# Stick-breaking prompt attention: where a unit's sigmoids stand against the copies of an older unit, and which unit carries the output projection

## The chip, the cores and the metric

The kernel runs on one core of one Trainium2 chip. The metric is device microseconds (us) of one execution. The engines named below are PE (TensorE, matrix products and transposes), DVE (VectorE), ACT (ScalarE), POOL (GpSimd) and SP (the queue that issues most DMAs). Each engine works through its own instructions in the order in which they were written for it; between engines there are only semaphores.

## The reference, cut to what matters

One step of a hybrid decoder layer: a prompt of 4096 tokens and eight short samples pass a common input projection, four branches (state space, short convolution, stick-breaking attention, attention to a memory), gates and an output projection. The change lies in the stick-breaking attention of the prompt (4 heads of 64, strictly causal):

```python
z = einsum("nqhd,nkhd->nhqk", q, k) * HEAD_DIM ** -0.5 + bias
log_beta = log_sigmoid(z)
log_1m = where(mask, log_sigmoid(-z), 0.0)
rev = cumsum(log_1m, axis=3, reverse=True)
excl = concatenate([rev[..., 1:], 0])
wts = where(mask, exp(log_beta + excl), 0.0)
out = einsum("nhqk,nkhd->nqhd", wts, v)
```

The kernel works without logarithms: a weight is sigmoid(z) times the product of sigmoid(-z) over all later keys, and that product is a scan from the last key to the first.

## The kernel before, in words

Up to about 1950 us the kernel projects the prompt and decodes the samples; that part is not touched. Then comes the attention loop. Its blocks are (query chunk of 512, head pair, key chunk of 512), from the diagonal key chunk backwards; each block has four *units* of 128 queries, in all 288 units. Of the 72 blocks 16 are diagonal, and their units have 128, 256, 384 and 512 keys; all others have 512. For unit `i` the loop body (lines 1882 to 1910) does, with `j = i - 3`:

- `scores(i)` (L1451, L1455): PE makes the scores z of both heads, six matmuls. The tag `z` has 4 buffers in PSUM, so two units' worth.
- background pieces (`run_bg`) and `out_step`: `run_bg` advances generators, of which `sample_gen` (the rest of the sample decoding, with its own transposes in the tag `wt`) is the largest; `out_step` advances the output projection `out_unit` (L1561 to L1563, tile `wo`). One step is six matmuls; after four steps half a tile of 128 tokens is done and DVE adds the residual (`yb`). Some 27 of the 32 tiles of 128 tokens are projected inside the loop, on average 1.5 steps for every two units. In `before` both run in odd units.
- `stage_b(j)` (L1489): PE transposes the weights of the older unit `j` (tag `wt`, 2 buffers in PSUM, one per head); the copy into `wT` is made by DVE for head 0 (L1492) and by ACT for head 1; every fourth unit ACT makes both. For those units `j` is even.
- `weights(i)`: for each head ACT makes `om` = sigmoid(-z) and `bt` = sigmoid(z), DVE scans `om` into `T` (L1472), POOL multiplies `bt` by `T` and, except in the last key chunk, copies the carry (`cy`, L1477). `om` has one buffer per head, `T` 4, `bt` 7.
- `run_norms`: the final norm of a projected tile, in pieces.
- `stage_c` (L1505): if `j` is even, so if `i` is odd, PE multiplies the values with the weights of the two units before `j` (tile `ya`).

So every odd unit of `before` holds scores, projection, transposes and values on PE, every even unit only scores and transposes. The order of the Python calls is the order of the instructions on each engine; a buffer is handed on when the instructions that used it are done.

Of the kernel before, what the change touches and what calls it, by code (L numbers as in the profile page):

```python
# [29 lines left out]
def hymba_kernel(ctx: ExitStack, tc: tile.TileContext, x_p, x_s, cache_k, cache_v, s_re, s_im, s_conv,  # L30
# [10 lines left out]
    def act(out, in_, f=AF.Copy, **kw):  # L41
        return S.activation(out, in_, f, **kw)  # L42

    def tt(eng, out, a, b, op):
        return eng.tensor_tensor(out=out, in0=a, in1=b, op=op)  # L45
# [58 lines left out]
    def run_bg(skip=None):  # L104
        for g in list(bg):
            if g is not skip and next(g, "end") == "end":
                bg.remove(g)
# [1011 lines left out]
    def load_q(qc, hp):  # L1119
        t = x_tile("qst", F32R).rearrange("p (l n) -> p l n", l=2)  # L1120
        SP.dma_start(t.bitcast(F32), qscr[:, hp * 128:(hp + 1) * 128, qc * 512:(qc + 1) * 512].rearrange("l p n -> p l n"))
        qst_t[qc, hp] = t
# [186 lines left out]
    i = 0  # L1309
# [96 lines left out]
    def load_kv(*b):  # L1406
        load_keys(*b, sb.tile([128, 2, 512], F32R, tag="kst", name="kst", bufs=2))
        load_v2(*b)
# [8 lines left out]
    def wout_gen():  # L1417
        for k in range(KT):
            stg = sb.tile([128, DM], F32, tag="x2", name="stg2", bufs=2)
            SP.dma_start(stg, w_out[0, k * 128:(k + 1) * 128, :])  # L1420
            act(wo[:, k, 0, :], stg)
            tt(V, wo[:, k, 1, :], stg, wo[:, k, 0, :].bitcast(F32), ALU.subtract)
            yield
# [17 lines left out]
    def scores(qc, hp, kb, qt):  # L1441
        ks = kst_t[qc, hp, kb]
        diag = kb == qc
        n = (qt + 1) * 128 if diag else 512

        qs = qst_t[qc, hp]
        zs = [ztile() for h in range(2)]
        for lq_, lk in ((0, 0), (0, 1), (1, 0)):
            for h in range(2):
                r = slice(64 * h, 64 * h + 64)  # L1450
                mm(zs[h][:, 0:n], qs[r, lq_, qt * 128:(qt + 1) * 128], ks[r, lk, 0:n],  # L1451
                   start=(lq_ + lk == 0), stop=(lq_ == 1 and not diag))
        if diag:
            for h in range(2):
                mm(zs[h][:, n - 128:n], idr, maskr, start=False, stop=True)  # L1455
        return zs, n

    def weights(zs, n, qc, hp, kb, qt):
        diag = kb == qc
        ws = []  # L1460
        for h in range(2):
            z, hd = zs[h], 2 * hp + h
            om = om2[h]
            T = sb.tile([128, 513], F32, tag="T2", name="T2", bufs=4)
            c = cy[:, 2 * qt + h:2 * qt + h + 1]
            bt = sb.tile([128, 512], F32, tag="bt2", name="bt2", bufs=7)
            act(om[:, 0:n], z[:, 0:n], AF.Sigmoid, scale=-0.125, bias=nb4[:, hd:hd + 1])
            act(bt[:, 0:n], z[:, 0:n], AF.Sigmoid, scale=0.125, bias=b4[:, hd:hd + 1])
            if n < 512:
                V.memset(om[:, n:n + 1], 1.0)  # L1470

            V.tensor_tensor_scan(T[:, 0:n + 1][:, ::-1], om[:, 0:n + 1][:, ::-1],  # L1472
                                 z[:, 0:1].to_broadcast([128, n + 1]), 1.0 if diag else c,
                                 op0=ALU.mult, op1=ALU.bypass)
            tt(P, bt[:, 0:n], bt[:, 0:n], T[:, 1:n + 1], ALU.mult)
            if kb:
                P.tensor_copy(c, T[:, 0:1])  # L1477
            ws.append(bt)
        return ws, n
# [3 lines left out]
    def stage_b(qt, ws, n):  # L1483

        for h in range(2):
            t = wtp()
            cnt[0] += 1
            for k in range(n // 128):
                tr(t[:, k, :], ws[h][:, k * 128:(k + 1) * 128], ident)  # L1489
            if qt % 2 == 0:  # L1490
                wts[h] = sb.tile([128, 4, 2, 128], F32, tag="wT2", name="wT2", bufs=4)
            (act if h or cnt[0] % 8 == 1 else V.tensor_copy)(wts[h][:, 0:n // 128, qt % 2, :], t[:, 0:n // 128, :])  # L1492
        return dict(wts)

    def stage_c(qc, hp, kb, qt, wTs):

        if kb == qc and qt == 1:
            ya[0] = ps.tile([128, 512], F32, tag="ya", name="ya", bufs=1)
        v = vt_t[qc, hp, kb]
        nk = qt + 1 if kb == qc else 4  # L1500
        for k in range(nk):

            q0 = qt if kb == qc and k == nk - 1 else qt - 1
            for h in range(2):
                mm(ya[0][h * 64:h * 64 + 64, q0 * 128:(qt + 1) * 128], v[:, k, h * 64:h * 64 + 64],  # L1505
                   wTs[h][:, k, q0 - qt + 1:2, :].rearrange("p a b -> p (a b)"),
                   start=(kb == qc and qt == 1 and k == 0), stop=(kb == 0 and k == nk - 1),
                   skip_group_check=True)
        if kb == 0 and qt == 3:
            y = Yc.setdefault(qc, sb.tile([128, 2, 512], F32, tag="Yc", name="Yc", bufs=1) if hp == 0 else None)  # L1510
            act(y[:, hp, :], ya[0])
            sq = sb.tile([128, 512], F32, tag="sq2", name="sq2", bufs=2)
            act(sq, ya[0], AF.Square)
            sqs2.append(sq)
            if hp == 1:
                bg.append(merge_c(qc, y, list(sqs2)))
                sqs2.clear()
# [78 lines left out]
    def run_norms():  # L1596
        for g in list(nrm):
            if next(g, "end") == "end":
                nrm.remove(g)
# [12 lines left out]
    def out_step(n):  # L1612

        ost["acc"] += n
        while ost["acc"] >= 1.0:
            if ost["gen"] is None:
                if ost["nxt"] is None:
                    out_ready()
                    ost["acc"] = min(ost["acc"], 1.0)
                    return ost["nxt"] is not None  # L1620
                ost["gen"], ost["nxt"] = ost["nxt"], None
                if not ost["split"]:
                    next(ost["gen"])
                ost["split"] = False
                out_ready()
            ost["acc"] -= 1.0
            ost["done"] += 1
            if ost["done"] % 8 == 6 and ost["nxt"] is not None and not ost["split"]:
                next(ost["nxt"])
                ost["split"] = True  # L1630
            if next(ost["gen"], "end") == "end":
                ost["gen"] = None
            if ost["done"] % 4 == 0 and not ost.get("tail"):
                break
        return True
# [240 lines left out]
    units = [(qc, hp, kb, qt) for (qc, hp, kb) in blocks for qt in range(4)]  # L1876
    nu = len(units)
    smp = sample_gen()
    bg.append(smp)
    sa, sbq = {}, {}  # L1880
    LAG = 3
    for i in range(nu + LAG + 1):
        j = i - LAG
        z = None
        if i < nu:
            qc, hp, kb, qt = units[i]
            if qt == 0:
                bi = i // 4
                if bi + 1 < len(blocks):
                    load_kv(*blocks[bi + 1])  # L1890
                    if blocks[bi + 1][:2] != (qc, hp):
                        load_q(*blocks[bi + 1][:2])
            z = scores(*units[i])
        if i == 5:
            bg.append(wout_gen())

        if i % 2 or i < 20:
            run_bg(smp if i < 10 or i % 2 == 0 else None)
        if i < nu:
            if i % 2:  # L1900
                out_step(max(0.0, 8.0 * (4 * NCH - 5) - ost["done"]) * 2 / (nu - i + 1))

        if 0 <= j < nu:
            ws, n = sa.pop(j)
            sbq[j] = stage_b(units[j][3], ws, n)
        if z is not None:
            sa[i] = weights(*z, *units[i])
        run_norms()
        if j >= 2 and j % 2 == 0:
            stage_c(*units[j - 1], sbq[j - 1])  # L1910
# [46 lines left out]
```

## Time and profile before

| what | value |
|---|---|
| median of three runs | 3369.91 us (3361.84 to 3379.39) |
| the profiled execution | 3368.33 us |
| its span | 3366.6 us, so 1.7 us lie around it |
| mean granted TensorE clock | 0.977 |
| PE busy over the span | 3155.7 us (94%) |
| DVE, ACT, POOL busy | 2290.5 (68%), 1783.4 (53%), 1267.8 us (38%) |

Durations below are read from the one profiled execution. In the timeline a row gives the start, the length, the engine, the line and operation, the tile written and read, how many instructions were merged, and in brackets the idle time before it with what ended it. A matmul's end is modelled; the distance between the starts of two groups tells what a group cost.

### The profile page before, as it was taken

Reading aid. Unit: us, or ns where it says so; the run is one execution under the profiler, and the core shown is the slowest. Engines: PE = TensorE matmul, PEld = TensorE weight load, DVE = VectorE, ACT = ScalarE, POOL = GpSimd, SP = SyncE. Lnnn points to the kernel's source line nnn. Section 1 sums busy time; section 2 is a strip of 40 time slices with the busy share of each in tenths; the row PEclk is TensorE's granted clock in tenths of the full one; section 3 lists DMA queues with packets and bytes.
Section 4 is the critical chain, followed back from the end, with each engine's and each line's share of the span. In section 5 each row is a group of like instructions: output and inputs, shape, how many; then the busy total and the mean of one; then the engine's idle time right before and its main releaser. Section 6 shows DMA issues by size and latency. Waiting matters only on the chain. (4 is left out here: it accounts for less than half of the span.)

```text
span 3366.6 us, 64925 instructions
## 1 busy us (share of the span) xinstructions
PE 3155.7 (94%) x23191; PEld 2260.2 (67%) x23191; DVE 2290.5 (68%) x3659; ACT 1783.4 (53%) x3324; POOL 1267.8 (38%) x1721
## 2 busy tenths in 40 slices
PE   7888999999999999999999978999999998999998
PEld 6556767677767677776677656666676665666667
DVE  5876667666676676676756567777767777677773
ACT  3435444443544444444434456667656666677771
POOL 1466422222222122222223035555545455555550
PEclk9999999999999999999999989999999999999999
DMA  6667887888887879878887443333333233322213
GB/s 212 193 209 235 276 276 227 270 280 268 277 262 244 283 250 299 266 234 271 270 276 223 147 160 122 97 97 92 98 94 96 72 106 101 96 77 85 87 60 119
DMA packets 382178, 623.55 MB, mean 185 GB/s; under 512 B 54568, under 2 KB 245488, under 8 KB 381856
## 3 DMA queue, kind: packets, MB, share of 16 engines
q1 hardware_dynamic: 344912, 484.90, 45.8%
q0 software_dynamic: 36944, 134.50, 12.1%
q8 instruction: 185, 3.03, 0.4%
q14 instruction: 137, 1.12, 0.1%
HBM read 539.33 MB, written 79.95 MB: 184 GB/s over the span
## 5 line engine op out<-in xcount | busy, mean ns | idle before, releaser
L45 POOL TENSOR_TENSOR bt<-bt,T 128x512 f32<-128x512 f32 (+3 forms) x576 | 603.3, 1047 | 605.7 <-DVE T L1472 416.5
L215 PE MATMUL pj<-xh,whl 128*128 128x512 f32 (+1 forms) x1792 | 725.0, 405 | 0.0
L1472 DVE TENSOR_TENSOR_SCAN T<-om,cy,z 128x513 f32<-128x513 f32 x448 | 549.7, 1268 | 231.5 <-ACT bt L42 100.4
L217 PE MATMUL pj<-xh,whl 128*128 128x512 f32 (+1 forms) x1792 | 659.8, 368 | 8.2 <-DVE whl L45 8.2
L216 PE MATMUL pj<-xh,whl 128*128 128x512 f32 (+1 forms) x1792 | 657.2, 367 | 0.1
L890 POOL DMA_INDIRECT kt<-in_cache_sb_k_dram,idxk x256 | 299.7, 1171 | 890.9 <-DVE kT L1058 790.5
L215 PEld LDWEIGHTS pj<-xh,whl 128*128 128x128 f32 x1792 | 344.5, 192 | 118.1 <-issue 79.8
L42 ACT ACTIVATE wT<-wt 128x512 f32<-128x512 f32 (+3 forms) x360 | 195.2, 557 | 408.1 <-PE wt L1489 407.9
L217 PEld LDWEIGHTS pj<-xh,whl 128*128 128x128 f32 x1792 | 343.9, 192 | 69.3 <-DVE whl L45 11.5
L42 ACT ACTIVATE bt<-z,b 128x512 f32<-128x512 f32 (+3 forms) x576 | 385.1, 669 | 0.0
L42 ACT ACTIVATE om<-z,nb 128x512 f32<-128x512 f32 (+3 forms) x576 | 380.4, 660 | 2.7 <-PE z L1455 2.1
L216 PEld LDWEIGHTS pj<-xh,whl 128*128 128x128 f32 x1792 | 346.2, 193 | 45.4 <-issue 8.6
L1451 PE MATMUL z<-kst,qst 64*128 64x512 f32 (+3 forms) x1704 | 325.2, 423 | 54.1 <-DVE T L1472 51.8
L1489 PE MATMUL wt<-ident,bt 128*128 128x128 f32 x2112 | 299.6, 281 | 34.9 <-ACT wT L42 8.0
L1058 DVE STREAM_TRANSPOSE kT<-kt 128x1024 f32<-128x1024 f32 x256 | 315.2, 1233 | 12.7 <-DMA kt<-in_cache_sb_k_dram,idxk 11.8
L1489 PEld LDWEIGHTS wt<-ident,bt 128*128 128x128 f32 x2112 | 241.5, 143 | 105.4 <-issue 52.2
L45 DVE TENSOR_TENSOR whl<-stg,whl 128x1024 fp32r<-128x1024 f32 x191 | 233.8, 1224 | 106.9 <-ACT whl L42 105.5
L1451 PEld LDWEIGHTS z<-kst,qst 64*128 64x128 f32 x1704 | 160.6, 187 | 176.5 <-DVE T L1472 95.0
L1505 PE MATMUL ya<-wT,vt 128*64 128x256 f32 (+1 forms) x2176 | 263.2, 383 | 0.3 <-DVE wT L1492 0.3
L42 ACT ACTIVATE whl<-stg 128x1024 fp32r<-128x1024 f32 x192 | 203.1, 1058 | 83.1 <-issue 34.9
L1561 PE MATMUL wo<-wo,mt 128*128 128x512 f32 x512 | 217.9, 426 | 2.3 <-ACT mt L42 2.3
L1563 PE MATMUL wo<-wo,mt 128*128 128x512 f32 x512 | 204.7, 400 | 1.0 <-DVE mt L45 1.0
(755 smaller groups left out, 4848.6 us busy)
## 6 DMA issues: line engine op xcount, KB each, us to landing
vt<-in_cache_sb_v_dram SPq DMA_DIRECT2D x1024, 128.0 KB
stg<-in_w_in_dram SPq DMA_DIRECT2D x192, 512.0 KB
kst<-kscr SPq DMA_DIRECT2D x71, 512.0 KB
xt<-in_x_prompt_dram SPq DMA_DIRECT2D x64, 512.0 KB
pkt<-pack_d SPq DMA_DIRECT2D x64, 449.0 KB
vt<-vscr SPq DMA_DIRECT2D x71, 256.0 KB
mr<-mscr SPq DMA_DIRECT2D x32, 512.0 KB
out_dram<-yb SPq DMA_DIRECT2D x32, 512.0 KB
```

The lines of the kernel that those rows point to most:

```text
L42: return S.activation(out, in_, f, **kw)
L45: return eng.tensor_tensor(out=out, in0=a, in1=b, op=op)
L215: mm(o[:, t0:t1], hi[:, k, :], xh[:, k, 0, t0:t1], start=(k == 0), stop=False)
L216: mm(o[:, t0:t1], hi[:, k, :], xh[:, k, 1, t0:t1], start=False, stop=False)
L217: mm(o[:, t0:t1], lo[:, k, :], xh[:, k, 0, t0:t1], start=False, stop=(k == KT - 1))
L890: P.indirect_dma_start(out=kq[j], out_offset=None, in_=ck_rows, in_offset=bass.IndirectOffsetOnAxis(ap=idxk[:, u // NU, gg:gg + 1], axis=0))
L1058: V.transpose(kts[j], kq.pop(j))
L1451: mm(zs[h][:, 0:n], qs[r, lq_, qt * 128:(qt + 1) * 128], ks[r, lk, 0:n], start=(lq_ + lk == 0), stop=(lq_ == 1 and not diag))
L1472: V.tensor_tensor_scan(T[:, 0:n + 1][:, ::-1], om[:, 0:n + 1][:, ::-1], z[:, 0:1].to_broadcast([128, n + 1]), 1.0 if diag else c, op0=ALU. ...
L1489: tr(t[:, k, :], ws[h][:, k * 128:(k + 1) * 128], ident)
L1505: mm(ya[0][h * 64:h * 64 + 64, q0 * 128:(qt + 1) * 128], v[:, k, h * 64:h * 64 + 64], wTs[h][:, k, q0 - qt + 1:2, :].rearrange("p a b -> p ...
L1561: mm(o, mt[:, k, 0, :], wo[:, k, 0, cs], start=(k == 0), stop=False)
```

## The change

In the loop body the background pieces and the output projection move from odd units to even ones; the values stay in odd units. And `weights(i)`, with its sigmoids, scans and products, is called before `stage_b(j)`, with its transposes and copies, instead of after it. Nothing is added or removed; every number of buffers stays.

```diff
-        if i % 2 or i < 20:
-            run_bg(smp if i < 10 or i % 2 == 0 else None)
+        if i % 2 == 0 or i < 20:
+            run_bg(smp if i < 10 or i % 2 else None)
         if i < nu:
-            if i % 2:
+            if i % 2 == 0:
                 out_step(max(0.0, 8.0 * (4 * NCH - 5) - ost["done"]) * 2 / (nu - i + 1))
-
+        if z is not None:
+            sa[i] = weights(*z, *units[i])
         if 0 <= j < nu:
             ws, n = sa.pop(j)
             sbq[j] = stage_b(units[j][3], ws, n)
-        if z is not None:
-            sa[i] = weights(*z, *units[i])
         run_norms()
         if j >= 2 and j % 2 == 0:
             stage_c(*units[j - 1], sbq[j - 1])
```

The places shown are in the last query chunk, in blocks off the diagonal. First ACT; the numbers behind the names tell one buffer's use from another, and a semaphore in brackets names the engine that is waited for. Before, from the copies of an odd unit on:

```order
L42 ACTIVATE wT2_35435<-wt_35430 128x4x128 [waits PE_49]
L42 ACTIVATE wT2_35442<-wt_35437 128x4x128 [waits PE_49]
L42 ACTIVATE om2_0_23883<-z_35409,nb4_87 128x512 [waits DVE_49]
L42 ACTIVATE bt2_35445<-z_35409,b4_86 128x512 [waits Pool_49]
L42 ACTIVATE om2_1_23884<-z_35410,nb4_87 128x512 [waits DVE_49]
L42 ACTIVATE bt2_35452<-z_35410,b4_86 128x512 [waits Pool_49]
```

Now, an even unit (z 35369 and 35370, with the transposes wt 35410 and 35416 of the unit three older) and the start of the odd one:

```order
L42 ACTIVATE om2_0_23883<-z_35369,nb4_87 128x512 [waits DVE_49,PE_49]
L42 ACTIVATE bt2_35397<-z_35369,b4_86 128x512 [waits Pool_49]
L42 ACTIVATE om2_1_23884<-z_35370,nb4_87 128x512 [waits DVE_49,PE_49]
L42 ACTIVATE bt2_35404<-z_35370,b4_86 128x512 [waits PE_49,Pool_49]
L42 ACTIVATE wT2_35361<-wt_35416 128x4x128 [waits PE_49]
L42 ACTIVATE om2_0_23883<-z_35422,nb4_87 128x512 [waits DVE_49,PE_49]
```

The four sigmoids stood behind the copies and stand ahead of them now; the second `bt` has a wait for PE that it did not have.

DVE at the same place, before: an even unit, then an odd one whose copies are both ACT's (the two rr rows belong to a background piece):

```order
L1492 COPY wT2_35346<-wt_35382 128x4x128 [waits PE_49]
L1472 SCALAR_TENSOR_TENSOR T2_35394<-om2_0_23883,cy_23887,z_35374 128x513 [waits DVE_49,Activation_49]
L1472 SCALAR_TENSOR_TENSOR T2_35401<-om2_1_23884,cy_23887,z_35375 128x513 [waits DVE_49,Activation_49]
L286 TENSOR_REDUCE rr2_35420<-rt_35417 128x4 [waits PE_49]
L288 TENSOR_SCALAR rr2_35420<-rr2_35420 128x4 [waits DVE_49]
L1472 SCALAR_TENSOR_TENSOR T2_35444<-om2_0_23883,cy_23887,z_35409 128x513 [waits Activation_49,Pool_49]
L1472 SCALAR_TENSOR_TENSOR T2_35451<-om2_1_23884,cy_23887,z_35410 128x513 [waits Activation_49,Pool_49]
```

and now, an even unit (T 35396, 35403), an odd one whose copies are both ACT's, and the next even one with the addition `yb` of the projection:

```order
L1472 SCALAR_TENSOR_TENSOR T2_35396<-om2_0_23883,cy_23887,z_35369 128x513 [waits Activation_49,Pool_49]
L1472 SCALAR_TENSOR_TENSOR T2_35403<-om2_1_23884,cy_23887,z_35370 128x513 [waits Activation_49,Pool_49]
L1492 COPY wT2_35355<-wt_35410 128x4x128 [waits PE_49]
L1472 SCALAR_TENSOR_TENSOR T2_35430<-om2_0_23883,cy_23887,z_35422 128x513 [waits Activation_49,Pool_49]
L1472 SCALAR_TENSOR_TENSOR T2_35437<-om2_1_23884,cy_23887,z_35423 128x513 [waits Activation_49,Pool_49]
L45 TENSOR_TENSOR yb_35298<-wo_35299,xt2_34808 128x512 [waits DMAHW7_49,PE_49]
L1472 SCALAR_TENSOR_TENSOR T2_35485<-om2_0_23883,cy_23887,z_35470 128x513 [waits DVE_49,Activation_49,Pool_49]
L1472 SCALAR_TENSOR_TENSOR T2_35492<-om2_1_23884,cy_23887,z_35471 128x513 [waits DVE_49,Activation_49,Pool_49]
L1492 COPY wT2_35449<-wt_35499 128x4x128 [waits PE_49]
```

The copy of a unit's transposes stood ahead of its two scans and stands behind them; `yb` stands ahead of an even unit's scans.

PE before, an odd unit: scores, projection, transposes (the values follow):

```order
L1451 MATMUL z<-kst,qst 128x512 [waits DVE_49] x2
L1451 MATMUL z<-kst,qst 128x512 x4
L1561 MATMUL wo<-wo,mt 128x512
L1562 MATMUL wo<-wo,mt 128x512
L1563 MATMUL wo<-wo,mt 128x512
L1561 MATMUL wo<-wo,mt 128x512
L1562 MATMUL wo<-wo,mt 128x512
L1563 MATMUL wo<-wo,mt 128x512
L1489 MATMUL wt<-ident,bt_35395 128x128 [waits DVE_49,Pool_49]
L1489 MATMUL wt<-ident,bt_35395 128x128 x3
L1489 MATMUL wt<-ident,bt_35402 128x128 [waits Activation_49,Pool_49]
L1489 MATMUL wt<-ident,bt_35402 128x128 x3
```

and now, the end of an even unit (projection, transposes) and an odd one (scores, transposes, values):

```order
L1562 MATMUL wo<-wo,mt 128x512
L1563 MATMUL wo<-wo,mt 128x512
L1489 MATMUL wt<-ident,bt_35235 128x128 [waits DVE_49,Pool_49]
L1489 MATMUL wt<-ident,bt_35235 128x128 x3
L1489 MATMUL wt<-ident,bt_35242 128x128 [waits DVE_49,Pool_49]
L1489 MATMUL wt<-ident,bt_35242 128x128 x3
L1451 MATMUL z<-kst,qst 128x512 x6
L1489 MATMUL wt<-ident,bt_35307 128x128 [waits Activation_49,Pool_49]
L1489 MATMUL wt<-ident,bt_35307 128x128 x3
L1489 MATMUL wt<-ident,bt_35314 128x128 [waits DVE_49,Pool_49]
L1489 MATMUL wt<-ident,bt_35314 128x128 x3
L1505 MATMUL ya<-wT_35355,vt_34892 64x256
```

The scores lose their own wait for DVE. Between the transposes of an even unit and those of the odd unit after it there are now only six score matmuls, and the second four transposes of the odd unit wait for DVE.

## Rows read from the trace of the kernel before

**Rows 1.** Windows: stretch, busy us of PE, PEld, DVE, ACT, POOL, clock, DMA.

```profile
1958.00:2050.00 92.00, 70.74 (x392) 45.77 (x393) 59.28 (x102) 60.10 (x126) 42.14 (x58) 0.78 0.51 168
2050.00:3290.00 1240.00, 1165.88 (x7485) 793.99 (x7484) 903.06 (x1159) 842.95 (x1532) 678.52 (x1004) 0.99 0.29 90
```

**Rows 2.** Waits, 1980 to 3290 us: total us, times, longest.

```profile
ACT wT L42 <- PE wt L1489: 404.8, 270, 9.3
DVE T L1472 <- ACT bt L42: 141.7, 107, 3.4
...
PE z L1451 <- DVE T L1472: 51.5, 143, 1.2
```

**Rows 3.** Timeline of PE, one pair of units late in the loop.

```profile
3203.65 0.97 PE L1451 MATMUL z<-kst,qst 64*128 64x512 f32 x6
...
3204.55 1.09 PE L1489 MATMUL wt<-ident,bt 128*128 128x128 f32 x8
...
3205.57 0.50 PE L1451 MATMUL z<-kst,qst 64*128 64x512 f32 x1
...
3206.23 0.96 PE L1451 MATMUL z<-kst,qst 64*128 64x512 f32 x5 [0.16 <-DVE T L1472]
...
3207.12 0.50 PE L1561 MATMUL wo<-wo,mt 128*128 128x512 f32 x1
...
3208.62 1.03 PE L1489 MATMUL wt<-ident,bt 128*128 128x128 f32 x8
...
3209.58 1.95 PE L1505 MATMUL ya<-wT,vt 128*64 128x256 f32 x16
...
3211.46 0.96 PE L1451 MATMUL z<-kst,qst 64*128 64x512 f32 x6
```

**Rows 4.** Timeline of ACT and DVE, same pair.

```profile
3202.94 0.69 ACT L42 ACTIVATE bt<-z,b 128x512 f32<-128x512 f32 x1
...
3203.72 2.46 DVE L1472 TENSOR_TENSOR_SCAN T<-om,cy,z 128x513 f32<-128x513 f32 x2 [1.59 <-ACT bt L42]
...
3209.25 1.09 ACT L42 ACTIVATE wT<-wt 128x512 f32<-128x512 f32 x2 [0.66 <-PE wt L1489]
```

**Rows 5.** Timeline of DVE and PE, an odd unit with a sample piece.

```profile
2700.02 2.44 DVE L1472 TENSOR_TENSOR_SCAN T<-om,cy,z 128x513 f32<-128x513 f32 x2
...
2701.16 0.60 PE L1489 MATMUL wt<-ident,bt 128*128 128x128 f32 x4
...
2702.39 0.66 DVE L1801 COPY g<-wt 128x512 f32<-128x512 f32 x1
...
2702.97 0.68 DVE L1492 COPY wT<-wt 128x512 f32<-128x512 f32 x1
...
2703.19 0.63 PE L1489 MATMUL wt<-ident,bt 128*128 128x128 f32 x4 [1.43 <-DVE g L1801]
...
2703.75 1.95 PE L1505 MATMUL ya<-wT,vt 128*64 128x256 f32 x16
```

**Rows 6.** Timeline: transposes and the addition of a projected half.

```profile
2121.70 1.03 PE L1489 MATMUL wt<-ident,bt 128*128 128x128 f32 x8
2121.89 0.69 DVE L45 TENSOR_TENSOR yb<-wo,xt 128x512 f32<-128x512 f32 x1 [1.04 <-PE wo L1563]
```

**Rows 7.** Timeline of PE: an odd unit's scores, after a pair with short values.

```profile
3169.64 0.49 PE L1451 MATMUL z<-kst,qst 64*128 64x512 f32 x1 [0.39 <-DVE T L1472]
...
3171.71 0.51 PE L1561 MATMUL wo<-wo,mt 128*128 128x512 f32 x1
```

**Rows 8.** Timeline of PE: late second transposes of odd units, first and last.

```profile
2113.93 0.63 PE L1489 MATMUL wt<-ident,bt 128*128 128x128 f32 x4 [0.78 <-ACT wT L42]
...
3036.16 0.63 PE L1489 MATMUL wt<-ident,bt 128*128 128x128 f32 x4 [1.11 <-POOL cy L1477]
```

**Rows 9.** Windows as in rows 1; a projection step's start and end.

```profile
2600.00:2620.00 20.00, 17.05 (x90) 11.22 (x86) 15.64 (x18) 10.89 (x20) 10.03 (x10) 0.83 0.35 118
2840.00:2860.00 20.00, 16.46 (x110) 10.72 (x110) 15.06 (x22) 14.61 (x27) 10.41 (x17) 1.00 0.49 155
...
2341.40 0.78 PE L1561 MATMUL wo<-wo,mt 128*128 128x512 f32 x1
...
2343.83 1.04 PE L1489 MATMUL wt<-ident,bt 128*128 128x128 f32 x8
```

## The prediction, made before the changed kernel ran

> **What bounds the kernel now.** I read the windows first, then the waits, then the timeline of single pairs of units. Off the attention loop the two programs are alike, so only the loop counts. Its steady stretch of 1240 us has PE busy for 1166, DVE for 903, ACT for 843 and POOL for 679 [rows 1]. PE is the engine to watch, but no engine is full, so the order decides. Of the waits, ACT's copies wait 405 us in all for PE's transposes, and what stands behind these copies on ACT, the four sigmoids, waits with them; DVE's scans wait for the last `bt` sigmoid; and at the end of this chain PE waits 143 times for a scan before it may write scores [rows 2]. The timeline tells what one such time costs: the pair of units at 3203.65 spends 0.90 us on the even unit's scores, 1.02 on its transposes, 1.55 on the odd unit's scores, 1.50 on one projection step, 0.96 on transposes and 1.88 on values, together 7.81 [rows 3]. The odd scores start, stop after one matmul for the scan that frees their buffer and go on: 0.65 us more than the even ones. Without that the pair is 7.16.
>
> **What goes.** Sigmoids no longer stand behind copies that wait for the projection, so the scans of a unit are over long before the scores two units later want its buffer. The even unit's scans now end about 3 us after its transposes start (below), the scores that want them come 6 us after. 143 x 0.65 = 93 us go [rows 2, 3]. After the 14 pairs with short values (a block behind a diagonal one) the odd scores are longer, 2.07 from start to projection instead of 1.55 [rows 7]: 14 x 0.5 = 7. Together 100.
>
> The second thing that goes is a collision with the sample pieces. Before, such a piece sits in an odd unit; PE transposes for it, but DVE comes to copy only after the even unit's two scans, and meanwhile the piece holds one of the two `wt` buffers. In the example the second transposes start at 2703.19, 2.03 us after the first, where 0.49 would do [rows 5]. There are 30 such odd units (late by 0.4 us or more), the first and the last in [rows 8]; summed over them PE loses 29 us. Now the piece sits in an even unit, at a time when DVE has done the odd unit's copy and waits for the next sigmoids (by steps like those below, some 1.7 us). I let 29 go, and also 12 for even units whose transposes came 0.4 us or more late (18 of them, the same way of counting), and 10 for projection steps that ran at the lower clock behind such gaps (2.43 instead of 1.50 in the example [rows 3, 9]). These 51 are the softest numbers here; I leave 12 of them standing, since some pieces have waits of their own. So 100 + 39 = 139 us go.
>
> **What comes.** The wait to price is the new one in the ACT rows of the change. `bt` has 7 buffers and a unit takes two. Calling `weights(i)` before the transposes of unit i-3 makes eight live, so the second `bt` of every unit waits until PE has transposed head 0 of unit i-3. Queued behind that sigmoid are ACT's copy and, through the scan of head 1, DVE's copy of head 0; and for this copy waits the second half of the next unit's transposes. In an even unit PE has only six score matmuls in between. Step by step, from the start of the even unit's transposes:
>
> - to ACT's start: 0.63 (3208.62 to 3209.25 [rows 3, 4])
> - sigmoid: 0.69, and 0.09 to the scan (3203.63 to 3203.72 [rows 4])
> - scan of head 1, to the start of what follows on DVE: 1.17 (two scans take 2.37 to the next start, 2700.02 to 2702.39 [rows 5], the first about 1.20 of it)
> - copy 0.68; 0.14 from a copy's end to PE (2703.05 to 2703.19 [rows 5])
>
> Sum 3.40. Without waiting PE would be there after 0.97 (rest of the even transposes) + 0.90 (scores) + 0.51 (first half) = 2.38 [rows 3]. The wait is 1.02, and four transposes restarted after a wait take 0.56 until the values start instead of 0.51 [rows 5]: 1.06 us per pair. In the odd unit the same chain has 1.88 us of values, 0.90 of scores and 1.50 of projection as cover, 4.3 us, and costs nothing. A longer projection step doesn't help the even unit: the chain starts at its end.
>
> 288 units in 72 blocks, 16 of them diagonal, are 112 full pairs and 32 diagonal ones. 112 x 1.06 = 119 us. The second pair of a diagonal block has 384 keys in its even unit and a short transpose in the odd one: shorter sigmoid, scan and cover, by the same chain about 0.7; 16 x 0.7 = 11. The first pair has 128 keys: nothing.
>
> `yb`, moved along with the projection, stands ahead of the even unit's scans on DVE and waits for the last projection matmul: it starts 0.19 after the transposes and takes 0.69 [rows 6]. Then 0.88 + 1.20 + 1.17 + 0.68 + 0.14 = 4.07 instead of 3.40: 0.67 more. It happens twice for each of 27 tiles, by share 42 times in full pairs: 28 us. The subtraction for `mt`, the norm pieces and most sample pieces fall into DVE's gap between its copy and the next scans; if that cover is too short, they delay the scans as `yb` does, which I hold inside the 12 us above. DMAs, SP's queue and POOL's products keep their places; POOL has half its time free.
>
> **Sum**, against the profiled execution's own 3368.3 us (1.6 below the median of the runs): 3368.3 - 139 + 119 + 11 + 28 = 3387 us. A change of 0.5% (17 us) is about what a measurement of this kernel can tell from none, and the sum stands just at that edge. Bounds of what no row shows directly: the new wait could be 0.8 (scan and copy overlapping more) or 1.4 us (a late sigmoid) per pair, so 26 us less or 38 more; the soft 51 all gone or half left, 12 less or 14 more.
>
> **Rivals.**
>
> *The waits go and little comes in their place.* If the second `bt` did not hold up the scans, in a pair with one projection step (about half) DVE's copy would still be 0.7 late, 56 x 0.7 = 39, and with two steps in time: 3368 - 139 + 39 + 13 (half of the `yb` cost) = 3281. For it: PE's waits on scans are all of one kind, and these do go. Against it: seven buffers for eight live tiles, and the scan is seen to start right behind the `bt` sigmoid and not behind `om` [rows 4]. Chance 0.15.
>
> *One wait for another, and no change.* If the soft 51 go wholly and the `yb` cost is hidden wherever two steps are taken (half): 3387 - 12 - 14 = 3361, with the upper bound of the wait up to 3380. For it: the terms are of like size, and what they count is the same DVE and ACT work pushed from one buffer to the other. Against: `yb` always ends a call of the projection, so nothing hides it. Chance 0.23.
>
> *Slower, by the clock.* The clock granted to PE fell to 0.83 in a stretch with several waits in a row and stayed at 1.00 in another with PE busy for only 16.5 of 20 us [rows 9]. Now every pair holds a gap of about 1 us, with `yb` of 1.7. If half of the 144 pairs ran one step's length at the lower of the two levels (1.2 for 2.4 GHz) and lost 0.93 as the step shown [rows 3, 9], that is 67 us: 3454. Against: that second stretch; by these two rows it takes several gaps close together. Chance 0.12.
>
> [...]
>
> **How the numbers follow.** The forecast, 3387, has 0.50, with its own range 3365 to 3410: 0.22 of it within 0.5% and 0.28 above. The first rival (0.15) is faster, and 0.03 of the second; the rest of the second (0.20) is the same; the third (0.12) slower. Faster 0.18, same 0.42, slower 0.40. The range from 3320 to 3440 leaves out most of the first rival and half of the third, about 0.2.
>
> **What would show it.** In the new profile PE's waits for scans before scores should be gone, and the odd unit's transposes, 1.0 us long before, should take about 2.1, with their second half waiting for DVE's copy; the even unit's second `bt` should start 0.63 after the transposes start. Late in the loop, where the sample is done, a pair with one step should take 8.2 us instead of 7.8; the middle, from 2100 to 3030, should gain. The forecast is wrong if odd transposes stay at 1.0 (then the first rival), if the clock of the loop falls below 0.95 (the third), or if even units' transposes begin to wait, which I took to be free.

## The result, and the profile after

The changed kernel takes 3430.8 us (median; 3419.1 to 3434.9), the kernel before 3369.0 in the same series: ratio 1.0175, 95% interval 1.0153 to 1.0196. The forecast was 3387 with an own range up to 3410, so the direction of the sum was right and its size too small by 44 us. The profiled execution took 3433.7 us, its span is 3431.9.

First the windows of the changed kernel, columns as in [rows 1]. The last two stretches are ten us around a late pair and two pairs without one.

```profile
2050.00:3290.00 1240.00, 1084.82 (x7112) 736.11 (x7112) 870.47 (x1117) 822.77 (x1466) 623.34 (x963) 0.98 0.29 88
...
3066.00:3076.00 10.00, 6.61 (x34) 3.97 (x33) 8.90 (x9) 5.16 (x11) 4.76 (x7) 0.71 0.22 84
3244.00:3262.00 18.00, 15.66 (x110) 10.18 (x108) 13.12 (x15) 13.52 (x23) 10.60 (x19) 1.00 0.25 75
```

In the same 1240 us PE is busy for 1085 us, where it was 1166 [rows 1]; DVE, ACT and POOL do less too. So nobody is busier: everybody waits. The clock explains little of it: 0.98 against 0.99, by estimate 0.01 of 1240 us or some 12 us. Who waits for whom stands in the list of waits from 1980 to 3350 us (us in total, times, longest):

```profile
ACT bt L42 <- PE wt L1489: 184.7, 125, 3.9
PE wt L1489 <- DVE wT L1492: 147.7, 129, 3.8
...
DVE T L1472 <- ACT bt L42: 109.1, 86, 3.9
...
DVE yb L45 <- PE wo L1563: 102.2, 51, 5.8
...
DVE Yc L1533 <- DMA ev<-gscr: 21.2, 9, 4.8
```

The 143 waits of PE for a scan before scores [rows 2] are gone; no such line is left. In their place PE waits 129 times before transposes for DVE's copy, 1.1 us each time, and ACT 125 times before a `bt` sigmoid for transposes. How one hangs on the other shows in the timeline of the pair at 3244.45, with one step of projection, like that of [rows 3]:

```profile
3246.83 1.03 PE L1489 MATMUL wt<-ident,bt 128*128 128x128 f32 x8
3247.53 0.69 ACT L42 ACTIVATE bt<-z,b 128x512 f32<-128x512 f32 x1 [0.23 <-PE wt L1489]
3247.80 0.97 PE L1451 MATMUL z<-kst,qst 64*128 64x512 f32 x6
...
3248.31 1.28 DVE L1472 TENSOR_TENSOR_SCAN T<-om,cy,z 128x513 f32<-128x513 f32 x1 [0.21 <-ACT bt L42]
...
3248.85 0.63 PE L1489 MATMUL wt<-ident,bt 128*128 128x128 f32 x4
...
3249.51 0.67 DVE L1492 COPY wT<-wt 128x512 f32<-128x512 f32 x1
...
3250.32 0.63 PE L1489 MATMUL wt<-ident,bt 128*128 128x128 f32 x4 [0.84 <-DVE wT L1492]
...
3250.88 1.95 PE L1505 MATMUL ya<-wT,vt 128*64 128x256 f32 x16
...
3252.76 0.96 PE L1451 MATMUL z<-kst,qst 64*128 64x512 f32 x6
...
3255.13 1.03 PE L1489 MATMUL wt<-ident,bt 128*128 128x128 f32 x8
3255.33 0.69 DVE L45 TENSOR_TENSOR yb<-wo,xt 128x512 f32<-128x512 f32 x1 [2.72 <-PE wo L1563]
...
3255.94 2.45 DVE L1472 TENSOR_TENSOR_SCAN T<-om,cy,z 128x513 f32<-128x513 f32 x2
...
3259.11 0.63 PE L1489 MATMUL wt<-ident,bt 128*128 128x128 f32 x4 [1.33 <-DVE wT L1492]
```

Read it downwards: even transposes, second `bt` 0.70 later, scan of head 1, copy of head 0, second half of the odd transposes. From 3246.83 to 3250.32 this is 3.49 us. The odd transposes take 2.03 us from their start to that of the values (3248.85 to 3250.88) instead of 1.0; the pair takes 8.31 us instead of 7.81. In the next pair `yb` stands ahead of both scans; there the wait grows from 0.84 to 1.33 and the pair to 8.79. Pairs with two steps went from 9.2 to 9.7, with three from 10.6 to 11.0 (medians). Summed over 140 pairs the loop takes 1362.6 us (1975.4 to 3338.0), before 1300.7 (1972.6 to 3273.2): 61.9 of the 65.4 us between the two profiled executions lie here.

One kind of pair the forecast had put at next to nothing. Timeline around 3062.74, where a chunk is finished and its norm (`merge_c`) begins:

```profile
3066.43 0.75 DVE L1533 SCALAR_TENSOR_TENSOR Yc<-Yc,gnc,ev 128x512 f32<-128x512 f32 x1 [4.83 <-DMA ev<-gscr]
...
3067.85 0.75 DVE L1533 SCALAR_TENSOR_TENSOR Yc<-Yc,gnc,ev 128x512 f32<-128x512 f32 x1 [0.67 <-DMA ev<-gscr]
3068.53 2.45 DVE L1472 TENSOR_TENSOR_SCAN T<-om,cy,z 128x513 f32<-128x513 f32 x2
...
3071.43 0.88 PE L1489 MATMUL wt<-ident,bt 128*128 128x128 f32 x3 [3.14 <-DVE wT L1492]
...
3072.24 1.55 PE L1505 MATMUL ya<-wT,vt 128*64 128x256 f32 x8
```

A product that waits for a tile just ordered by DMA now stands ahead of an even unit's scans. The scans start more than 2 us late, PE waits 3.14 us, and then runs at the lower of its two levels: these values take 1.48 us to the next scores (3072.24 to 3073.72) where the same number took 0.80 elsewhere, and the window above shows 0.71. The lower level also stands behind shorter waits, as here, behind one of 1.39 us:

```profile
2540.96 0.38 PE L1489 MATMUL wt<-ident,bt 128*128 128x128 f32 x1 [1.39 <-DVE wT L1492]
2541.26 3.50 PE L1505 MATMUL ya<-wT,vt 128*64 128x256 f32 x16
```

These values take 3.44 us to the next scores, elsewhere 1.88. In sixteen odd units the values ran wholly or in part at the lower level, in the kernel before in three.

### The profile page after: what moved, and what is told of

Same layout as the page of the kernel before. It is cut to its first block, busy times and chain, and to the rows that moved or that the text cites. A ratio compares the mean times of both kernels' runs of the same rounds, so it can differ in the third digit from the quotient of the medians.

```text
span 3431.9 us, 65412 instructions
## 1 busy us (share of the span) xinstructions
PE 3122.5 (91%) x23191; PEld 2236.2 (65%) x23191; DVE 2303.4 (67%) x3659; ACT 1803.9 (53%) x3324; POOL 1241.7 (36%) x1721
## 3 DMA queue, kind: packets, MB, share of 16 engines
q14 instruction: 140, 1.15, 0.1%
## 5 line engine op out<-in xcount | busy, mean ns | idle before, releaser
L45 POOL TENSOR_TENSOR bt<-bt,T 128x512 f32<-128x512 f32 (+3 forms) x576 | 585.9, 1017 | 686.1 <-DVE T L1472 552.1
L1489 PE MATMUL wt<-ident,bt 128*128 128x128 f32 x2112 | 315.9, 281 | 180.0 <-DVE wT L1492 148.6
L42 ACT ACTIVATE bt<-z,b 128x512 f32<-128x512 f32 (+3 forms) x576 | 375.1, 651 | 189.3 <-PE wt L1489 184.7
L1505 PE MATMUL ya<-wT,vt 128*64 128x256 f32 (+1 forms) x2176 | 277.3, 398 | 0.3 <-DVE wT L1492 0.3
L1451 PE MATMUL z<-kst,qst 64*128 64x512 f32 (+3 forms) x1704 | 268.3, 420 | 1.6 <-DMA qst<-qscr 1.6
L1561 PE MATMUL wo<-wo,mt 128*128 128x512 f32 x512 | 213.8, 418 | 0.6 <-ACT mt L42 0.6
L1505 PEld LDWEIGHTS ya<-wT,vt 128*64 128x64 f32 x2176 | 150.8, 143 | 90.5 <-issue 34.9
L1563 PE MATMUL wo<-wo,mt 128*128 128x512 f32 x512 | 201.2, 393 | 0.5 <-DVE om L1470 0.5
L1562 PE MATMUL wo<-wo,mt 128*128 128x512 f32 x512 | 200.9, 392 | 0.0
```

What stands on the lines that cost most here:

```text
L1561: mm(o, mt[:, k, 0, :], wo[:, k, 0, cs], start=(k == 0), stop=False)
```

## The experiments

Times are medians, ratios are to the kernel before, measured beside each, with 95% intervals. Runs of different series are compared by their ratios.

**Each half alone.** `parity` moves projection and pieces to the even units and leaves `stage_b` ahead of `weights`; `order` puts `weights` ahead and leaves projection and pieces in odd units.

> Only the projection and the pieces move to the unit without values; transposes and copies stay ahead of the sigmoids, as before. Theory (each half alone costs, and the two are joined by the order on ACT): the even unit's sigmoids now wait behind copies that come only after the projection, so the scans end about 1 us too late for the scores two units later, in every pair; 3400 to 3480 us, PE waiting for scans before scores in 250 or more places. Rival (the place of the projection matters little, all of the loss is in the new order of sigmoids and copies): 3360 to 3380 us.

> Only the sigmoids, scans and products go ahead of the transposes and copies; projection and pieces stay in the unit with values. Theory (what costs is that the second bt of the even unit waits for transposes that stand behind the projection): here these transposes follow the scores at once, the second bt hardly waits, and a pair with two steps of projection covers the chain; 3320 to 3385 us, odd transposes late by 1.1 to 1.6 us only in pairs with one step. Rival (DVE's copy behind its scans costs the same with either place of the projection): 3415 to 3445 us.

`parity`: 3361.3 us, 0.9970 (0.9954 to 0.9986). `order`: 3346.1 us, 0.9935 (0.9916 to 0.9954). So neither half costs; both gain a little, and only together they lose. For `parity` my theory was wrong: PE does wait for scans before nearly all even scores (first row below, 0.5 us each), but nearly all odd scores lost their wait, and the late transposes behind sample pieces are nearly gone. The time is the rival's, but its reason is not: the new order alone loses nothing. For `order` the theory held but for a size: the odd transposes wait in pairs with one step (the other rows, 0.63 us where 1.1 to 1.6 were expected; such pairs take 7.98) and not in pairs with two (8.51, against 9.2 before).

Waits of `parity`:

```profile
PEld z L1451 <- DVE T L1472: 77.4, 149, 1.1
```

Timeline of `order`, an odd unit's transposes, one step:

```profile
3225.69 0.60 PE L1489 MATMUL wt<-ident,bt 128*128 128x128 f32 x4
...
3226.11 0.66 DVE L1492 COPY wT<-wt 128x512 f32<-128x512 f32 x1
...
3226.91 0.63 PE L1489 MATMUL wt<-ident,bt 128*128 128x128 f32 x4 [0.63 <-DVE wT L1492]
```

**Eight buffers for `bt`.**

```diff
-        return sb.tile([128, 512], dt, tag="ev2", name=name, bufs=4)
+        return sb.tile([128, 512], dt, tag="ev2", name=name, bufs=3)
...
-            bt = sb.tile([128, 512], F32, tag="bt2", name="bt2", bufs=7)
+            bt = sb.tile([128, 512], F32, tag="bt2", name="bt2", bufs=8)
```

> The changed kernel with eight buffers for bt instead of seven (the tag ev2 gives one of its four for it). Theory (seven buffers for eight live tiles): the wait of the second bt for the transposes goes; a pair with one step gains the 0.23 us that ACT waited there, a pair with two steps, where the transposes come 1.5 us later, all of its 1.15: 3345 to 3385 us. Rival (the sigmoids, scans and copy in a row are too long by themselves, the buffer is incidental): 3405 to 3425 us, that is 112 x 0.23 = 26 us less at most.

3373.8 us, 1.0013 (1.0003 to 1.0023): 1.6% or 55 us of the loss go. The price per pair is as expected: with two steps 9.69 becomes 8.53, with three 11.05 becomes 9.89, with one 8.31 becomes 7.98 (medians); pairs with `yb` gain nothing (one step 8.80 and 8.81, two steps 10.2 and 10.4). A pair with two steps, timeline:

```profile
3188.85 2.45 DVE L1472 TENSOR_TENSOR_SCAN T<-om,cy,z 128x513 f32<-128x513 f32 x2
...
3189.22 0.70 ACT L42 ACTIVATE bt<-z,b 128x512 f32<-128x512 f32 x1
...
3190.27 1.03 PE L1489 MATMUL wt<-ident,bt 128*128 128x128 f32 x8
3191.23 0.66 DVE L1492 COPY wT<-wt 128x512 f32<-128x512 f32 x1
...
3192.13 1.09 PE L1489 MATMUL wt<-ident,bt 128*128 128x128 f32 x8
```

The second `bt` starts a microsecond before the transposes that it had to wait for, the copy follows both scans while PE makes the odd scores, and the odd transposes run in one piece. So the buffer is the whole wait with two steps, and about 0.3 of 1.15 us with one; there the two scans, one behind the other, still make the copy late. The list of waits also fits that neither half loses alone. In `order` the even transposes follow the scores at once, and no even unit's second `bt` waits for them; those of odd units do, 83 times and 140 us in all, where values and scores lie behind as cover. In `parity` the transposes of the older unit are issued ahead of the sigmoids, so eight buffers are never wanted, and no `bt` waits for transposes.

**The scan without the `bt` sigmoid.** The scan's second operand is never used (its operation is a bypass), but it is read from the scores, which the sigmoid reads too, and the scan starts only behind that sigmoid.

```diff
-                                 z[:, 0:1].to_broadcast([128, n + 1]), 1.0 if diag else c,
+                                 nb4[:, hd:hd + 1].to_broadcast([128, n + 1]), 1.0 if diag else c,
```

> The changed kernel, with the scan's unused second operand (its second operation is a bypass) taken from a column in SBUF instead of the scores in PSUM; by that the scan no longer waits for the bt sigmoid, only for om. Theory (scan 1 and DVE's copy hang on the second bt): without yb the copy comes 0.9 us sooner and the odd transposes wait 0.0 to 0.3 us instead of 0.84; where yb stands ahead of the scans nothing is gained; 70 x 1.15 + 16 us less: 3320 to 3355 us. Rival (the copy's place behind two scans is what costs, whatever they wait for): the scans start sooner but odd transposes still wait 0.7 us or more in pairs with one step, 3390 us or more. If the scan is slower with both operands in SBUF (1.28 us now), the gain shrinks by that.

3429.7 us, 1.0177 (1.0158 to 1.0196): nothing gained, the rival's number. But this tells little of the chain, since the edit brought a cost of its own. Window and timeline of this run:

```profile
2050.00:3290.00 1240.00, 1083.58 (x7107) 741.39 (x7104) 1012.48 (x1117) 825.11 (x1468) 976.82 (x960) 0.97 0.29 88
```

```profile
3238.09 2.13 POOL L45 TENSOR_TENSOR bt<-bt,T 128x512 f32<-128x512 f32 x1
...
3243.92 3.71 DVE L1472 TENSOR_TENSOR_SCAN T<-om,cy,nb 128x513 f32<-128x513 f32 x2
...
3244.38 1.12 POOL L1477 COPY cy<-T 128x1 f32<-128x1 f32 x1
...
3258.30 0.18 POOL L1477 COPY cy<-T 128x1 f32<-128x1 f32 x1
...
3258.44 2.45 DVE L1472 TENSOR_TENSOR_SCAN T<-om,cy,nb 128x513 f32<-128x513 f32 x2
...
3259.89 1.89 POOL L45 TENSOR_TENSOR bt<-bt,T 128x512 f32<-128x512 f32 x1 [1.41 <-DVE T L1472]
```

Beside a scan POOL's copy of one column takes 1.12 us instead of 0.18, and two scans take 3.71 us here and up to 4.34 elsewhere, instead of 2.45. In the last rows the scans take 2.45 as ever; there POOL's product, which begins beside them, takes 1.89 instead of 1.09. POOL's busy time rose from 623 to 977 us.

**Copy between the scans.** With seven buffers and `yb` in its place, only DVE's copy of head 0 is moved. PE's order stays.

```diff
+            if h == 0 and mid is not None:
+                mid()
...
-            sa[i] = weights(*z, *units[i])
+            sa[i] = weights(*z, *units[i], mid=copies)
```

(`copies` calls `stage_b` for the older unit; ACT's copies are issued after `weights`, as before.)

> The changed kernel, seven bt buffers, with DVE's copy of head 0 between the two scans instead of behind both; yb stays ahead. Theory (PE waits only for this copy; the second bt and the scan of head 1 may come late): the copy needs one scan and the transposes, so odd transposes are not late with one step or two, and 0.2 to 0.4 late with yb; 145 + 21 us of the odd scores and transposes go, 15 stay: 3265 to 3310 us. Rival (the scan of head 1, now behind the copy, comes late instead, and PE waits for scans before scores again): 3350 us or more.

3286.9 us, 0.9763 (0.9747 to 0.9780): 139 us below the changed kernel. This is the theory's number. Its waits:

```profile
ACT bt L42 <- PE wt L1491: 153.6, 119, 3.7
...
PE wt L1491 <- DVE wT L1499: 34.4, 61, 4.2
```

It settles the main point. The second `bt` waits nearly as often as in the changed kernel (119 times against 125), but PE's wait for the copy falls from 148 to 34 us: the second `bt` and the scan of head 1 may be late, what costs is the copy.

**`yb` behind scans and copy**: with seven buffers (`yb`), with eight (`bt8_yb`), and with the copy between the scans (`mid_yb`).

```diff
-            tt(V, yb[0:rows, cs], o[0:rows], xt[0:rows, cs], ALU.add)
+            def add(o=o, cs=cs, half=half):
+                tt(V, yb[0:rows, cs], o[0:rows], xt[0:rows, cs], ALU.add)
...
+        for f in later:
+            f()
```

> The changed kernel, seven bt buffers, copy behind both scans, and only yb moved behind scans and copy. This sizes the yb term alone, forecast as 42 x 0.67 = 28 us. Theory (with seven buffers yb falls partly together with the wait of the second bt, so it costs less here than the 55 us that it cost with eight): 20 to 35 us less than the changed kernel, 3396 to 3412 us. Rival (the terms add up, as if each stood alone): 50 us or more less, 3380 us.

> The changed kernel with eight bt buffers, and yb written on DVE behind the unit's scans and copy instead of ahead of them. In the run with eight buffers alone pairs with yb stay at 8.80 us (one step) where those without take 7.98, and 10.40 against 8.53 with two steps. Theory (yb ahead of the scans pushes DVE's copy back, and with it the odd transposes): 36 x 0.8 + 17 x 1.2 + 9 us of diagonal pairs, 58 us less than 3374: 3305 to 3330 us. Rival (yb costs its own 0.67 us, whereever it stands, because DVE's row of scans and copy is full): 3350 to 3375 us.

> As the run before (copy between the scans, seven buffers), and yb behind scans and copy. Theory: the last 0.2 to 0.4 us of the pairs with yb go, and pieces of the scan delay in the pairs after them; 10 to 20 us below the run with the copy between the scans. Rival (yb there is already hidden): the same within 5 us.

`yb`: 3394.4 us, 1.0075 (1.0058 to 1.0092), 34 us less than the changed kernel. `bt8_yb`: 3318.9 us, 0.9850 (0.9833 to 0.9867), 55 us less than with eight buffers alone, and its pairs with `yb` take 7.98 like those without. `mid_yb`: 3271.2 us, 0.9706 (0.9688 to 0.9724), 16 to 19 us less than `mid`. All three are as the theory had them (`yb` 2 us below its range): what `yb` costs depends on what else is late in that pair.

**The chunk norm's products two pieces later.**

```diff
+            sls.append(sl)
...
-            V.scalar_tensor_tensor(y[:, ft, :], y[:, ft, :], gnc[:, 4 + ft:5 + ft], sl, op0=ALU.mult, op1=ALU.mult)
         yield
+        yield
+        for ft in range(2):
+            V.scalar_tensor_tensor(y[:, ft, :], y[:, ft, :], gnc[:, 4 + ft:5 + ft], sls[ft], op0=ALU.mult, op1=ALU.mult)
```

> The changed kernel alone but for one thing: in the norm of a finished chunk the two products with the tile that a DMA has just been told to fetch (Yc, line 1533) come two pieces later, so DVE doesn't wait for that DMA ahead of an even unit's scans. Theory (these products, seven of them in the loop, hold the scans 2 to 4 us each time and lower the clock behind): 15 to 30 us less, 3400 to 3416 us. Rival (the gap moves on with the piece, or the pair would be late anyway): 3425 to 3435 us.

3403.4 us, 1.0101 (1.0084 to 1.0118): 25 us less. The line of DVE waiting for that DMA is gone from the list of waits; the changed kernel had nine such waits. But the edit does more than it was meant to: the finished chunk is ready one piece later, and by that projection steps move between pairs, in 94 of the 140. Their sum stays (214 steps, 53 `yb`), and most pairs of a kind cost the same as in the changed kernel (8.31 with one step, 8.81 with `yb`, 9.68 with two), so I put the gain down to the products; a run that tells the two apart is missing.

**All three, and two variants of it.** `mid_yb_merge` joins the last three edits. `best2` puts the background pieces behind the unit's copies as well. `mid_old_place` is `mid_yb_merge` with projection and pieces in odd units, as before the change.

> Copy of head 0 between the scans, yb behind them, and the chunk norm's two products two pieces later. Theory (in every earlier version a product that waits for its DMA on DVE is ahead of scans): 10 to 25 us less than 3271: 3246 to 3262 us. Rival (with the copy between the scans there is slack, the product is hidden): 3265 to 3275 us.

> As mid_yb_merge, and the background pieces of a unit come behind its sigmoids, scans, transposes and copies instead of ahead of them. Theory (sample pieces hold sigmoids on ACT and scans on DVE by their own waits for DMAs and PE): another 10 to 25 us less, 3225 to 3250 us. Rival (behind the copies they hold the next unit's sigmoids just as much): the same as mid_yb_merge within 5 us.

> As mid_yb_merge (copy between the scans, yb behind, products later), but projection and pieces in the units with values, as before the change. It tells what the new place of the projection is worth once the copy no longer waits. Theory (PE's waits are nearly gone in both, so the place matters little): 3245 to 3275 us, within 10 us of mid_yb_merge. Rival (with all of PE's work in one unit the copies of the other come late): 3290 us or more.

`mid_yb_merge`: 3249.2 us, 0.9646 (0.9629 to 0.9664), the fastest of all. Its pair at 3076.91, with one step and `yb`, in the timeline:

```profile
3079.30 1.03 PE L1491 MATMUL wt<-ident,bt 128*128 128x128 f32 x8
3079.99 0.69 ACT L42 ACTIVATE bt<-z,b 128x512 f32<-128x512 f32 x1 [0.24 <-PE wt L1491]
...
3080.47 0.66 DVE L1499 COPY wT<-wt 128x512 f32<-128x512 f32 x1
...
3081.05 1.27 DVE L1472 TENSOR_TENSOR_SCAN T<-om,cy,z 128x513 f32<-128x513 f32 x1
...
3081.28 1.06 PE L1491 MATMUL wt<-ident,bt 128*128 128x128 f32 x8
...
3082.24 0.66 DVE L45 TENSOR_TENSOR yb<-wo,xt 128x512 f32<-128x512 f32 x1
```

and in its waits:

```profile
ACT bt L42 <- PE wt L1491: 158.3, 116, 4.2
...
PE wt L1491 <- DVE wT L1499: 21.5, 25, 2.9
```

The second `bt` still waits 116 times, 158 us in all, and it costs next to nothing, since PE's wait for the copy fell from 148 to 21 us. The pair takes 7.24 us; the wait-free one was worked out as 7.16.

`best2`: 3296.6 us, 0.9778 (0.9761 to 0.9794); both expectations were wrong, it is 47 us slower than `mid_yb_merge`. `mid_old_place`: 3351.3 us, 0.9939 (0.9921 to 0.9958), the rival's number; its pairs without pieces are as short as those of `mid_yb_merge` (medians 7.24, 8.51, 9.9), so the loss is in those with pieces. A timeline of one of them:

```profile
2705.56 1.28 DVE L1472 TENSOR_TENSOR_SCAN T<-om,cy,z 128x513 f32<-128x513 f32 x1 [2.41 <-issue]
...
2706.76 0.66 DVE L1499 COPY wT<-wt 128x512 f32<-128x512 f32 x1
...
2707.48 0.64 PE L1827 MATMUL sms<-g,g 128*32 128x256 f32 x8 [1.39 <-DVE wT L1499]
```

A sample piece needs one of the two `wt` buffers and gets it only when DVE has copied the transposes of the unit before. In the odd unit nothing but scores lies between these transposes and the piece. In the even unit of the changed kernel the values lie there too. `best2` makes the same mistake in another way: its pieces follow right behind their own unit's transposes, and its list of PE's waits shows the same kind of line:

```profile
PE wt L1740 <- DVE wT L1499: 8.6, 12, 1.2
PE wt L1755 <- DVE wT L1499: 5.8, 7, 1.6
```

## Why the forecast fell short, by its own steps

- **Scores waiting for scans, -100.** Right: the line is gone from the list of waits.
- **The chain, +119 for full pairs.** Place and mechanism were right, and in the pair shown the sum came within 0.1 us: second `bt` after 0.70 (0.63 forecast), sum 3.49 instead of 3.40, 1.15 us a pair instead of 1.06. (1.02 and 0.05 make 1.07, and a wait of 0.8 would be 29 us less, not 26; neither matters.) The 112 pairs make 10 us of that. What the prediction had only half right is the reason: it put the whole wait on the seven buffers. By the run with eight, they make all of it in pairs with more steps and a third with one; the place of the copy behind two scans makes the rest.
- **`yb`, +28.** 34 us when it alone is moved: some 6 us too small.
- **"The subtraction for `mt`, the norm pieces and most sample pieces fall into DVE's gap", at most 12 us together with all that stays of the collisions.** This step failed. The gap on DVE before the scans is real, but an instruction that stands in it with a wait of its own doesn't fill the gap, it stretches it. The products of the chunk norm wait for a DMA issued in the same piece; the run that moves these gives back 25 us. Only 12 had been allowed for all such places together.
- **Collisions with pieces, -51, of which 12 stay.** This held as far as it can be counted. From start to start, over the 140 pairs, the even transposes take 16 us less than before (12 forecast) and the projection steps 10 us less (10 forecast). The 29 us of late odd transposes can't be told from the chain in the changed kernel; in `parity` odd transposes are late by 0.1 us on the mean. What remains in the changed kernel is of another kind (the point above, and some pairs in which `mt` of the sample or sample products hold a sigmoid or scan by 2 to 4 us; these were not tried alone).
- **Diagonal pairs, +11.** Their odd transposes lose some 20 us, since `yb` falls on nine of the fifteen counted; part of that is in the `yb` run's 34.
- **The clock of the values, put at nothing outside its rival.** Values take 260 us over the 140 pairs, 246 before. These 14 us belong to the sixteen odd units at the lower clock; `merge` has six of them, and its values take 249. So part of what `merge` gains is clock.

Of the 44 us that were missing, the chain makes 10, `yb` 6 and the norm's products 25; but 12 of these 25 were in the 3387 already, as what was left standing, and the collisions seem to have gone wholly. That makes 10 + 6 + 13 = 29. The measured differences are uncertain by some 10 us each, and the part ahead of the loop, which no edit touches, differs by up to 17 us between profiled executions (the loop starts at 1950.4 us in `yb`, at 1967.6 in `merge`). Counted over the 140 pairs alone, `yb` is 39 us shorter than the changed kernel and `merge` 37. Then the same sum is 10 + 11 + 25 = 46, for the 43 that the loop lacks. This is agreement within what these runs can tell, not proof that nothing else counts, and the terms may overlap.

The first rival (waits go, little comes) had as its condition that the second `bt` doesn't hold up the scans. `bt8` makes that true and takes 3374, not 3281: the copy 0.7 late with one step came as it had it, but `yb` cost 55 us instead of 13, and the products stayed. That `mid` comes to 3287 is another order's doing. The second rival's 3361 to 3380 lies below what was measured. The clock rival falls for the loop as a whole: 0.98, and 1.00 over pairs that each hold a wait of 0.8 to 1.3 us. But it had a grain of truth: sixteen odd units, and against the rival's reading that it takes several gaps close together, a single wait of 1.39 us stood ahead of the values at 2541.26.

## What to carry to other kernels

Ask of each engine's queue which instruction another engine really waits for, and put it ahead of all that merely has to be done: one copy moved past one scan was worth 139 us, while a sigmoid that waited 116 times cost next to nothing. Where an instruction is moved ahead in a queue, go through everything that comes with it and has a wait of its own, above all for a DMA that was ordered just before. And two edits that each gain can lose together, when one lengthens the very interval that the other makes somebody wait for, so measure them apart.

## What the hardware showed that I had not expected

In `free`, a scan with both operands in SBUF and POOL's instructions hold each other up: POOL's one-column copy went from 0.18 to 1.12 us and its product in one place from 1.09 to 2.13, two scans from 2.45 to 3.71. With one operand in PSUM, in the changed kernel, they run side by side: no scan of the stretch takes over 1.28 us, and the median copy 0.18. The Trainium skill (SBUF — State Buffer, SBUF: two separate sides) says that a VectorE instruction with two SBUF inputs and a GpSimd instruction that reads SBUF take turns on a shared pair of ports, each for its whole length; the rows agree. The one thing that the edit changed is an operand whose value nobody uses: where it lies counts all the same.
